# Second group's gate operands in four lots behind four outputs of the first group, its sums of squares behind the fourth and the spread behind the sixth, in a hybrid decoder step on one Trainium2 core

## The chip, the cores and the metric

The program runs on one core of a Trainium2 chip. The metric is the device time of one execution in microseconds (us). All data are float32; matrix products are made of three products of float32r pieces each (high times high, high times low, low times high), so that one float32 product of 128x128 weights costs three matmuls.

## What is computed

One layer of a hybrid decoder for 1024 new prompt tokens and 64 sample tokens. The change touches only its last part, the gated per-layer embedding:

```
gate = sigmoid(rmsnorm(x, g_ple) @ w_ple_gate)     # x: 1088 tokens x 1024, w_ple_gate: 1024 x 1024
x = x + gate * (p @ w_ple_proj)                    # p: 1088 x 256, w_ple_proj: 256 x 1024
```

The result x is an output of the step (y_prompt, y_sample).

## The kernel before

The tokens are held transposed (features on the partitions) in two groups: A with tokens 0 to 511 and B with tokens 512 to 1087 (576 tokens, two halves of 288). Each group has eight tiles of 128 features in `x`. rmsnorm is not applied to x itself: the gain goes into the operand, and 1/rms of each token (the row `rb`, spread over the partitions) is multiplied onto the product afterwards, in `gated` (L1599).

**Group A's gate.** `gate` (L1635) takes a slice of 256 output features at a time, four slices, two outputs (tiles of 128 features) each: 8 outputs. An output is 24 matmuls of 512 columns into one of three accumulator banks (0, 1, 2 in turn), then `gated`: 6 matmuls of the projection into bank 3 or 4 in turn (L1094 to L1096 with `ph`, `pl`), on VectorE the product with `rb` (L1603, which frees the accumulator bank), on ScalarE the sigmoid (L1604), on VectorE the product with the projection (L1605, which frees bank 3 or 4) and the sum into x (L1606). Last comes the store of the output before: four transposes on TensorE into bank 6 (L1615), a copy `yt` by ScalarE (L1616) and a DMA (L1617). The last slice's two outputs are made in halves of their inner dimension (L1638 to L1643).

**Group B's gate** (`gate7`, L1670) uses seven products of block sums instead of eight (`seven`, L1443). It needs operands made of B's x: four that are sums and differences of blocks (ids 2, 3, 1, 4; L1383 to L1399) and three direct ones (11, 21, 22; L1374 to L1382), and `rb` of B. For each k of 0 to 3 the four block operands cost two scalings on ScalarE (L1385, into `hk`), four subtractions on VectorE (L1390, L1392, L1394, L1396, into `tk`), four casts to the high piece on ScalarE (L1398) and four low pieces (L1399), two on VectorE and two on GpSimd (POOL). `rb` of B comes from `squares` (L1326: eight squares on ScalarE, three additions on POOL and three on VectorE, L1333, and one last one, L1334) and `spread` (L1337: products with a column of ones, L1345, square root, reciprocal, products that spread it, L1354). The direct operands are put where A's own operands `nh`, `nl` stood, so they wait for A's last matmul. `ple_inputs` (L1585) brings B's p: five DMAs `pn`, transposes (L1593), pieces `ph`, `pl` (L1596, L1597). `gate7_weights` (L1657) makes sums of weight blocks on VectorE (L1437 to L1440) and pieces of them (ScalarE L1074, then POOL or VectorE L1075).

**What sets the order.** The order on every engine comes from a list scheduler in the framework, which follows program order and its own estimates. The block `with tc.issue_after(end.ins)` (L1701) adds one rule: what is written in it for the engine of `end` (VectorE, the sum L1606 of output m) stands on that engine behind `end`. ScalarE's and POOL's instructions in the block are not bound by it. The loop of L1700 runs over the eight outputs of group A, m = 0 to 7, and hangs B's preparation behind them. Each engine works through its own list in order; SP issues the DMAs in its own list's order.

Of the kernel before, what the change touches and what calls it, by code (L numbers as in the profile page):

```python
# [48 lines left out]
def hybrid_step(ctx: ExitStack, tc: tile.TileContext, I, O):  # L49
# [17 lines left out]
    def banks(*ids):  # L67

        turn = itertools.cycle(ids)

        def take():
            i = next(turn)
            return psum.tile([128, 512], F32, name=f"b{i}", bufs=1)

        return take
# [152 lines left out]
    for s in range(2):  # L228
        hs = slice(64 * s, 64 * s + 64)
        for q in range(2):  # L230
            for kind in range(2):
                m = mfull[hs, q, kind, :]
# [1313 lines left out]
    mpb = tc.alloc_tile_pool(name="mlp_b", bufs=1, side="right", reuse_waits="tile")  # L1546
    B = Part(mpb, mpb, mpb, 512, 576, ((0, 288), (288, 288)))
# [14 lines left out]
    ops = B.operands("g_mlp", (2, 3, 1, 4), mpb, 4)  # L1562
# [22 lines left out]
    def ple_inputs(p, bank):  # L1585
        p.p = [[p.act(f"p{e}", F32R)] for e in "hl"]
        for i in p.tiles:
            r = 128 if i < 8 else NS
            t = B.tmp("pn")[:, :256]
            SP.dma_start(t[:r], pp_in[i * 128:i * 128 + 128, :] if i < 8 else ps_in)  # L1590
            pt = bank()
            for k in range(2):
                PE.transpose(pt[:, k * 128:k * 128 + r], t[:r, k * 128:k * 128 + 128], ident[:r, :r])  # L1593
            p3 = pt[:, :256].rearrange("p (k t) -> p k t", k=2)[:, :, :r]
            dst = slice(i * 128 - p.t0, i * 128 - p.t0 + r)
            S.copy(p.p[0][0][:, :, dst], p3)  # L1596
            V.tensor_sub(p.p[1][0][:, :, dst], p3, f(p.p[0][0][:, :, dst]))  # L1597
# [37 lines left out]
    def gate(p, sl):  # L1635
        w = load(wg_[:, sl * 256:sl * 256 + 256], 8, 256)
        w2_ = load(wp_[:, sl * 256:sl * 256 + 256], 2, 256)
        if sl == 3:  # L1638

            ps_ = [acc() for _ in range(2)]  # L1640
            for ks in (range(0, 4), range(4, 8)):
                for m2 in range(2):
                    gemm_p(ps_[m2], w, m2, p.h, 0, p.n, ks=ks)  # L1643
        for m2 in range(2):
            for t0, n in p.chunks:
                if sl == 3:
                    ps = ps_[m2]
                else:
                    ps = acc()
                    gemm_p(ps, w, m2, p.h, t0, n)  # L1650
                end = gated(p, w2_, m2, 2 * sl + m2, t0, n, ps[:, :n], B.tmp("g")[:, :n])
            finish(p, 2 * sl + m2)
            yield end
# [3 lines left out]
    def gate7_weights(sl, w):  # L1657

        s_ = [A.act("s", F32) for _ in range(2)]
        raw = [None] * 2 if sl % 2 == 0 else [B.act("wr", F32).rearrange("p a t -> p (a t)")[:, :1024] for _ in range(2)]  # L1660
        t = block_sums(wg_, sl * 256, [s_[i // 2][:, i % 2] for i in range(4)], raw)
        rp = raw_weights(wp_, 0, 2, sl * 256, 256, A.tmp("wr"))
        for n, i in enumerate((11, 2, 3, 1, 12, 4, 22) if sl else (2, 3, 1, 22, 11, 12, 4)):
            w[i] = split_piece(t[i], (G, V)[n % 2])
            if n == 6:
                w["p"] = Pieces(2)
                w["p"].hl[0, 0] = split_piece(rp, V)
            yield
# [30 lines left out]
    ops = {}  # L1699
    for m, end in enumerate(itertools.chain.from_iterable(gate(A, sl) for sl in range(4))):  # L1700
        with tc.issue_after(end.ins):  # L1701
            if m < 3:
                B.operands("g_ple", (2, 3, 1, 4), mpb, 4, ks=((0, 1), (2,), (3,))[m], out=ops)
            if m == 2:
                sums = B.squares()
            if m == 4:
                B.spread(sums, banks(3, 4))
                ple_inputs(B, banks(5, 7))
        if m == 6:
            w = {}  # L1710
            pieces = gate7_weights(0, w)
            for _ in range(5):
                next(pieces)
# [38 lines left out]
```

## Time and profile before

| | us |
|---|---|
| median of 3 runs | 1703.72 |
| lowest and highest run | 1699.27, 1712.79 |
| the profiled execution, its own time | 1706.69 |
| span of its trace, first to last instruction | 1705.1 |
| TensorE busy in the span | 1637.8 |

The span is the profiled execution from its first to its last instruction; 1.6 us of the execution's time lie outside it. Times in the trace count from the start of the span. TensorE (PE) rows give a matmul's busy time; matmuls overlap by a part, so the distance from start to start is what one costs: 0.23 us for 512 columns at the full clock. POOL is GpSimd, DVE is VectorE, ACT is ScalarE. A number in brackets behind a row is the time for which the engine stood idle just before it, with what ended that.

### The profile page before, as it was taken

To read this page: it belongs to the slowest core of one execution; us is meant where nothing else is said; L and a number is where in the kernel's file an instruction comes from. 1 tells how busy PE (TensorE), PEld (TensorE's weight loads), DVE (VectorE), ACT (ScalarE), POOL (GpSimd) and SP (SyncE) were. 2 spreads that over 40 slices of the span, in tenths; PEclk is the share of its full clock that TensorE was granted. 3 is DMA by queue.
4 is the path that set the end of the run, shared out by engine and by line. 5 is a ranking of instruction groups with operands and counts; after the bars stand their busy time and mean duration, and the time that the engine had idled before them with its cause. 6 is when DMAs were issued, how large, how long until landed. Compare 5 with 4: busy or idle time off the path is not lost.

```text
span 1705.1 us, 30847 instructions
## 1 busy us (share of the span) xinstructions
PE 1637.8 (96%) x11853; PEld 1476.2 (87%) x11853; DVE 1105.0 (65%) x1918; ACT 820.7 (48%) x1627; POOL 727.3 (43%) x778
## 2 busy tenths in 40 slices
PE   6999899999899889999999999999999999999898
PEld 5899888889898767888887778987999999999698
DVE  6266844555277759888854345378777777764986
ACT  6633433343343657666543444364444334436753
POOL 4123121123232664443434654366655445538621
PEclk9999999999999999999999999999999999999999
DMA  5134466325523763433245665322322222323232
GB/s 189 49 120 124 142 166 178 72 78 158 160 66 96 226 170 124 137 121 116 78 121 149 187 178 189 112 84 77 97 90 87 87 87 90 98 76 105 87 120 56
DMA packets 212372, 202.26 MB, mean 119 GB/s; under 512 B 58305, under 2 KB 177761, under 8 KB 212098
## 3 DMA queue, kind: packets, MB, share of 16 engines
q1 hardware_dynamic: 202498, 179.33, 35.4%
q0 software_dynamic: 5120, 16.78, 3.3%
q10 hardware_dynamic: 4608, 4.20, 1.0%
q8 instruction: 93, 1.52, 0.4%
q14 instruction: 53, 0.43, 0.1%
HBM read 163.27 MB, written 36.98 MB: 117 GB/s over the span
## 4 chain that ended last, share of the span: by engine, by line
PE 76%; DVE 10%; DMA 6%; ACT 3%; issue 3%; SPq 2%; POOL 1%; ACTq 0%; DVEq 0%; POOLq 0%
PE b L1094 12%; PE b L1096 11%; PE b L1095 11%; PE b L1453 4%; PE b L1455 4%; PE b L1454 4%; PE b L169 3%; PE b L170 3%; PE b L171 3%; PE b L797 2%; PE b L795 2%; PE b L796 2%; PE b L942 2%; DMA wr<-in_w_in 1%; PE b L512 1%
## 5 line engine op out<-in xcount | busy, mean ns | idle before, releaser
L1075 POOL TENSOR_TENSOR wl<-wr,wh 128x512 fp32r<-128x512 f32 x182 | 255.1, 1411 | 265.5 <-ACT wh L1074 226.3
L1074 ACT CAST wh<-wr 128x512 fp32r<-128x512 f32 x308 | 187.9, 621 | 308.9 <-PE b L1095 198.0
L1522 DVE TENSOR_TENSOR x<-b,x 128x288 f32<-128x288 f32 (+1 forms) x384 | 199.2, 528 | 97.2 <-PE b L1096 86.0
L1094 PE MATMUL b<-ah,wh 128*128 128x288 f32 (+1 forms) x768 | 253.7, 331 | 3.2 <-DVE x L1522 2.1
L1096 PE MATMUL b<-ah,wl 128*128 128x288 f32 (+1 forms) x768 | 252.2, 328 | 0.0
L1095 PE MATMUL b<-al,wh 128*128 128x288 f32 (+1 forms) x768 | 252.0, 328 | 0.0
L1094 PEld LDWEIGHTS b<-ah,wh 128*128 128x128 f32 x768 | 144.5, 188 | 15.3 <-DVE x L1522 4.8
L1096 PEld LDWEIGHTS b<-ah,wl 128*128 128x128 f32 x768 | 144.5, 188 | 10.2
L1095 PEld LDWEIGHTS b<-al,wh 128*128 128x128 f32 x768 | 144.6, 188 | 9.3 <-DVE al L1426 0.3
L1094 PE MATMUL b<-nh,wh 128*128 128x512 f32 x320 | 129.1, 403 | 5.4 <-DVE x L1413 3.3
L795 PE MATMUL b<-wh,h_hi 128*128 128x256 f32 x432 | 127.4, 295 | 5.1 <-ACT sq L805 5.1
L1095 PE MATMUL b<-nl,wh 128*128 128x512 f32 x320 | 128.1, 400 | 0.0
L1096 PE MATMUL b<-nh,wl 128*128 128x512 f32 x320 | 127.7, 400 | 0.0
L797 PE MATMUL b<-wh,h_lo 128*128 128x256 f32 x432 | 126.8, 293 | 0.0
L796 PE MATMUL b<-wl,h_hi 128*128 128x256 f32 x432 | 124.7, 289 | 0.0
L1075 DVE TENSOR_TENSOR wl<-wr,wh 128x512 fp32r<-128x512 f32 x126 | 102.4, 815 | 26.4 <-ACT wh L1074 22.4
L159 POOL TENSOR_TENSOR wl<-wr,wh 128x1024 fp32r<-128x1024 f32 x26 | 64.6, 2500 | 123.0 <-ACT wh L158 118.0
L169 PE MATMUL b<-h_hi,wh 128*128 128x384 f32 (+1 forms) x336 | 115.1, 342 | 1.9 <-ACT xs L333 1.3
L170 PE MATMUL b<-h_lo,wh 128*128 128x384 f32 (+1 forms) x336 | 113.8, 339 | 0.3 <-DVE h_lo L201 0.3
L171 PE MATMUL b<-h_hi,wl 128*128 128x384 f32 (+1 forms) x336 | 112.5, 335 | 0.0
L922 DVE TENSOR_TENSOR_SCAN keep<-keep,onesq 128x128 f32<-128x128 f32 (+3 forms) x64 | 95.3, 1488 | 21.4 <-POOL keep L920 20.7
L1453 PE MATMUL b<-op,wh 128*128 128x288 f32 x320 | 95.0, 297 | 0.1
(437 smaller groups left out, 4450.6 us busy)
## 6 DMA issues: line engine op xcount, KB each, us to landing
wr<-in_w_up SPq DMA_DIRECT2D x64, 512.0 KB
wr<-in_w_down SPq DMA_DIRECT2D x64, 512.0 KB
wr<-in_w_in SPq DMA_DIRECT2D x26, 512.0 KB
wr<-in_w_out SPq DMA_DIRECT2D x16, 512.0 KB
wr<-in_w_ple_gate SPq DMA_DIRECT2D x16, 512.0 KB
xt<-in_x_prompt SPq DMA_DIRECT2D x8, 512.0 KB
stk_s<-sth ACTq DMA_DIRECT2D x32, 128.0 KB
stk_s<-stl SPq DMA_DIRECT2D x32, 128.0 KB
```

Of the source, the lines that this page charges most:

```text
L169: PE.matmul(ps[:, :n], wh[:, k, c], a, start=(k == 0), stop=False)
L170: PE.matmul(ps[:, :n], wh[:, k, c], b, start=False, stop=False)
L171: PE.matmul(ps[:, :n], wl[:, k, c], a, start=False, stop=(k == nk - 1))
L795: PE.matmul(o, a, w[0][:, k, :], start=(k == 0), stop=False)
L797: last = PE.matmul(o, b, w[0][:, k, :], start=False, stop=(k == 7))
L1074: S.copy(h3, src)
L1075: (sub or G).tensor_sub(l3, src, f(h3))
L1094: PE.matmul(ps[:, :n], w(0, k, m), a, start=(k == 0), stop=False)
L1095: PE.matmul(ps[:, :n], w(0, k, m), b, start=False, stop=False)
L1096: PE.matmul(ps[:, :n], w(1, k, m), a, start=False, stop=(k == nk - 1))
L1453: PE.matmul(o, wh[:, k], x[:, 0, k], start=k == 0, stop=False)
L1522: V.tensor_add(p.x[:, m, t0:t0 + n], ps[:, :n], p.x[:, m, t0:t0 + n])
```

## The change

Two things move in the loop over group A's outputs. The block operands of B for k = 0, 1, 2, 3 were written behind outputs 0 (k = 0 and 1), 1 and 2; now each k has an output of its own, 0 to 3. B's squares move from output 2 to output 3, and the spread and B's p from output 4 to output 5. Outputs are numbered from 0 here and below.

```
-            if m < 3:
-                B.operands("g_ple", (2, 3, 1, 4), mpb, 4, ks=((0, 1), (2,), (3,))[m], out=ops)
-            if m == 2:
+            if m < 4:
+                B.operands("g_ple", (2, 3, 1, 4), mpb, 4, ks=(m,), out=ops)
+            if m == 3:
                 sums = B.squares()
-            if m == 4:
+            if m == 5:
                 B.spread(sums, banks(3, 4))
                 ple_inputs(B, banks(5, 7))
```

Three places where the scheduled order differs follow. Numbers behind b are those of a bank's use: before, outputs 2, 3, 4, 5, 6, 7 accumulate in b_18273, b_18352, b_18423, b_18524, b_18595, b_18596; now outputs 2, 3, 5 have b_18257, b_18318, b_18468, and outputs 4, 6, 7 the same names as before.

VectorE from output 3's product with `rb` to output 4's, before (b_18378 is output 3's projection, tk belongs to the lot k = 3, s is a sum of weight blocks):

```order
L1603 TENSOR_TENSOR g<-b_18352,rb 128x512
L1399 TENSOR_TENSOR op_18151<-tk,op_18151 128x288
L1399 TENSOR_TENSOR op_18153<-tk,op_18153 128x288
L1333 TENSOR_TENSOR sums<-sums,sq 128x576
L1437 TENSOR_TENSOR s<-wr 128x512
L1439 TENSOR_TENSOR s<-wr 128x512
L1333 TENSOR_TENSOR sums<-sums,sq 128x576
L1605 TENSOR_TENSOR g<-b_18378,g 128x512
L1438 TENSOR_TENSOR s<-s,wr 128x512
L1333 TENSOR_TENSOR sums<-sums,sq 128x576
L1606 TENSOR_TENSOR x<-x,g 128x512
L1603 TENSOR_TENSOR g<-b_18423,rb 128x512
```

The same place now (b_18344 is output 3's projection):

```order
L1603 TENSOR_TENSOR g<-b_18318,rb 128x512
L1399 TENSOR_TENSOR op_18150<-tk,op_18150 128x288
L1605 TENSOR_TENSOR g<-b_18344,g 128x512
L1606 TENSOR_TENSOR x<-x,g 128x512
L1390 TENSOR_TENSOR tk<-hk 128x288
L1396 TENSOR_TENSOR tk<-hk 128x288
L1392 TENSOR_TENSOR tk<-hk,tk 128x288
L1394 TENSOR_TENSOR tk<-hk,tk 128x288
L1437 TENSOR_TENSOR s<-wr 128x512
L1333 TENSOR_TENSOR sums<-sums,sq 128x576
L1439 TENSOR_TENSOR s<-wr 128x512
L1399 TENSOR_TENSOR op_18151<-tk,op_18151 128x288
```

Output 3's L1605 and L1606 now stand two and three places behind its L1603 instead of seven and ten; the lot k = 3, the sums of squares and the weight sums come behind them.

TensorE at the store of output 2 (b_18389 before, b_18355 now; b_18449 is output 4's projection), before:

```order
L1094 MATMUL b_18524<-nh_17988,wh 128x512
L1095 MATMUL b_18524<-nl_17990,wh 128x512
L1096 MATMUL b_18524<-nh_17988,wl 128x512
L1615 MATMUL b_18389<-ident,x 128x128 x4
L1094 MATMUL b_18524<-nh_17988,wh 128x512
L1095 MATMUL b_18524<-nl_17990,wh 128x512
```

And now:

```order
L1096 MATMUL b_18449<-ph,wl 128x512
L1094 MATMUL b_18449<-ph,wh 128x512
L1615 MATMUL b_18355<-ident,x 128x128 x4
L1095 MATMUL b_18449<-pl,wh 128x512
L1096 MATMUL b_18449<-ph,wl 128x512
L1094 MATMUL b_18468<-nh_17988,wh 128x512
```

The store stands 11 matmuls earlier: inside output 4's projection instead of behind the first nine matmuls of output 5.

TensorE at the products of the spread with the column of ones (b_18469 before, b_18514 now; b_18561 and b_18505 are the store of output 4), before:

```order
L1094 MATMUL b_18596<-nh_17988,wh 128x512
L1095 MATMUL b_18596<-nl_17990,wh 128x512
L1345 MATMUL b_18469<-onesq,sums 128x1 x5
L1096 MATMUL b_18596<-nh_17988,wl 128x512
L1615 MATMUL b_18561<-ident,x 128x128 x4
L1593 MATMUL b_18491<-ident,pn 128x128 x2
```

And now:

```order
L1096 MATMUL b_18596<-nh_17988,wl 128x512
L1345 MATMUL b_18514<-onesq,sums 128x1 x2
L1615 MATMUL b_18505<-ident,x 128x128 x4
L1345 MATMUL b_18514<-onesq,sums 128x1 x3
L1094 MATMUL b_18596<-nh_17988,wh 128x512
L1095 MATMUL b_18596<-nl_17990,wh 128x512
```

Before, the products stand behind 11 matmuls of output 7, and output 5's six projection matmuls come only later; now they stand behind 6 matmuls of output 7, with output 5's projection already done, and the transposes of p come later.

## Rows read from the trace of the kernel before

**Rows 1.** The head of the page: the span, and each engine's busy time, share and instructions.

```profile
span 1705.1 us, 30847 instructions
PE 1637.8 (96%) x11853; PEld 1476.2 (87%) x11853; DVE 1105.0 (65%) x1918; ACT 820.7 (48%) x1627; POOL 727.3 (43%) x778
```

**Rows 2.** Waits of PE from 1545 us to the end: engine, line, what it waited for, us in total, times, longest us.

```profile
PE b L1615 <- DVE x L1606: 3.6, 2, 2.5
PE b L1615 <- ACT yt L1616: 2.6, 1, 2.6
PE b L1345 <- DVE g L1605: 2.3, 1, 2.3
```

**Rows 3.** Busy time by stretch: stretch, its length, then busy us and instructions of PE, weight loads, DVE, ACT and POOL, the granted clock of PE as a share of full speed, DMA share, GB/s.

```profile
1577.50:1592.70 15.20, 15.20 (x71) 12.57 (x70) 14.05 (x18) 10.48 (x20) 9.62 (x8) 1.00 0.27 87
1592.70:1618.90 26.20, 18.80 (x87) 14.65 (x85) 25.99 (x31) 18.63 (x37) 18.89 (x13) 1.00 0.31 91
1618.90:1637.00 18.10, 18.05 (x90) 15.97 (x91) 13.12 (x28) 12.09 (x25) 3.28 (x2) 0.81 0.47 149
1637.00:1680.00 43.00, 43.00 (x326) 42.47 (x325) 41.08 (x78) 22.72 (x47) 15.45 (x11) 1.00 0.27 77
```

**Rows 4.** PE by time (start us, us, instruction, idle before): the three standstills, a matmul of 512 columns behind the last of them, one later, and two of 288 columns.

```profile
1604.02 0.66 PE L1615 MATMUL b<-ident,x 128*128 128x128 f32 x4 [2.64 <-ACT yt L1616]
...
1613.31 0.63 PE L1615 MATMUL b<-ident,x 128*128 128x128 f32 x4 [2.46 <-DVE x L1606]
...
1618.95 1.87 PE L1345 MATMUL b<-onesq,sums 128*128 128x1 f32 x10 [2.35 <-DVE g L1605]
...
1623.39 0.63 PE L1095 MATMUL b<-nl,wh 128*128 128x512 f32 x1
...
1632.55 0.29 PE L1455 MATMUL b<-op,wl 128*128 128x288 f32 x1
1632.69 0.29 PE L1453 MATMUL b<-op,wh 128*128 128x288 f32 x1
```

**Rows 5.** The chain of waits that ended last, its pieces just ahead of the spread (start us, us, what).

```profile
1614.77 1.85 DVE sums L1334
1616.62 1.67 DVE wl L1075
1618.29 0.61 DVE g L1605
...
1618.95 1.87 PE b L1345 x10
```

**Rows 6.** DVE by time: instructions on SBUF tensors alone and beside POOL, then the two products and the sum that finish output 3.

```profile
1583.20 0.45 DVE L1396 TENSOR_TENSOR tk<-hk 128x288 f32<-128x288 f32 x1
...
1584.17 1.54 DVE L1390 TENSOR_TENSOR tk<-hk 128x288 f32<-128x288 f32 x1
...
1603.34 0.68 DVE L1603 TENSOR_TENSOR g<-b,rb 128x512 f32<-128x512 f32 x1
...
1609.94 0.75 DVE L1333 TENSOR_TENSOR sums<-sums,sq 128x576 f32<-128x576 f32 x1
1610.61 0.68 DVE L1605 TENSOR_TENSOR g<-b,g 128x512 f32<-128x512 f32 x1
...
1612.48 0.68 DVE L1606 TENSOR_TENSOR x<-x,g 128x512 f32<-128x512 f32 x1
```

**Rows 7.** POOL by time at the place of the second row of rows 6, then two of its groups by line between 1594.4 and 1617.8 us (busy us, mean ns, idle before and its releasers).

```profile
1583.67 3.19 POOL L1075 TENSOR_TENSOR wl<-wr,wh 128x512 fp32r<-128x512 f32 x2 [1.31 <-ACT wh L1074]
...
L1075 POOL TENSOR_TENSOR wl<-wr,wh 128x512 fp32r<-128x512 f32 x4 | 6.4, 1602 | 2.5 <-ACT wh L1074 2.5
L1399 POOL TENSOR_TENSOR op<-tk,op 128x288 fp32r<-128x288 f32 x4 | 4.2, 1074 | 0.0
```

**Rows 8.** ACT by time: a table load ahead of a sigmoid, a sigmoid, the third cast of the lot k = 3, a square, and the copy `yt` of output 1's store.

```profile
1577.98 1.28 ACT L1604 ACT_TABLE_LOAD   x1
...
1592.86 0.63 ACT L1604 ACTIVATE g<-g 128x512 f32<-128x512 f32 x1 [1.06 <-DVE g L1603]
...
1602.48 0.43 ACT L1398 CAST op<-tk 128x288 fp32r<-128x288 f32 x1 [0.53 <-DVE tk L1396]
1602.82 0.68 ACT L1331 ACTIVATE sq<-x 128x576 f32<-128x576 f32 x1
1603.40 0.56 ACT L1616 COPY yt<-b 128x512 f32<-128x512 f32 x1
```

**Rows 9.** SP by time: the loads of the weights that L1437 and L1439 sum.

```profile
1599.73 1.83 SPq L1068 DMA_DIRECT2D wr<-in_w_ple_gate  x2
```

**Rows 10.** Busy time by stretch, columns as in rows 3: two other places where the granted clock fell.

```profile
629.00:637.00 8.00, 4.75 (x14) 3.76 (x15) 4.09 (x4) 4.72 (x9) 8.00 (x6) 0.79 0.24 76
...
901.00:907.40 6.40, 5.53 (x37) 4.49 (x37) 1.11 (x2) 2.40 (x6) 2.37 (x3) 0.73 0.68 221
```

**Rows 11.** DVE by time behind the spread: the last direct operand, a weight sum, and output 6's product with `rb`.

```profile
1630.53 1.81 DVE L1380 SCALAR_TENSOR_TENSOR op<-x,par,op 128x288 fp32r<-128x288 f32 x4 [3.59 <-ACT op L1379]
1632.25 0.69 DVE L1437 TENSOR_TENSOR s<-wr 128x512 f32<-128x512 f32 x1
1632.85 0.69 DVE L1603 TENSOR_TENSOR g<-b,rb 128x512 f32<-128x512 f32 x1
```

## Prediction, made before the changed kernel had run

> **What bounds the kernel now.** I read the head of the page, then PE's waits in the last part, then busy time by stretch, then the chain of waits and the single engines' timelines. PE is busy for 1637.8 of 1705.1 us [rows 1], so over the whole span PE is the bound, and the change can only win where PE stands still or runs slowly. Around the change PE waits four times; three of the waits lie where group A's gate is computed: 2.64, 2.46 and 2.35 us [rows 2, 4], 7.45 us together. By stretch [rows 3], PE is full from 1577.5 to 1592.7, busy 18.80 of 26.20 us from there to 1618.9, full again behind that but with a granted clock of 0.81 for 18.1 us, which costs 0.19 x 18.1 = 3.4 us, and full at full clock from 1637 to 1680. That is what there is to win: 7.45 + 3.4 = 10.9 us, 0.6% of the time.
>
> In the stretch of the standstills another engine is full: DVE, 25.99 of 26.20 us [rows 3]. The chain of waits runs along DVE there and reaches PE through the last sum of squares (L1334), a weight piece and output 4's L1605, behind which the spread's first product starts at 1618.95 [rows 5]. So the stage is set by DVE up to that point, and PE's standstills are what is left over.
>
> **What DVE's time is made of.** In those 26.2 us DVE runs 29 instructions of interest: 13 of 288 columns (five L1399, eight subtractions), 12 of 512 (two L1603, three L1605, two L1606, four weight sums, one L1075) and 4 of 576 (three L1333, one L1334). Alone, one of 288 columns takes some 0.37 us from start to start (the L1396's 0.45 of rows 6 less the 0.07 by which a row's end overlaps the next start, as for L1605: 0.68 there, 0.61 in rows 5), one of 512 thus 0.61, one of 576 0.67 (L1333 to L1605 in rows 6). That is 13 x 0.37 + 12 x 0.61 + 4 x 0.67 = 14.8 us. The other 11.4 us are time in which DVE waits for POOL inside an instruction: an instruction on two SBUF tensors takes 1.54 instead of 0.45 us when POOL is in one of its own [rows 6, 7], and POOL is busy 18.89 us here with 13 instructions [rows 3].
>
> **The change part by part.** Nothing is added or removed; it is all order. Up to 1592.7 nothing moves on any engine: the lots k = 0 and 1 already ran together, because outputs 0 and 1 end together, and they still do.
>
> Between 1592.7 and the spread the same 29 DVE instructions and the same 13 of POOL run as before, only sorted differently. So the time at which DVE is through with L1334 and output 4's L1605 moves only by what DVE idles and by how the POOL waits fall. I find two new idles: output 2's and output 3's L1605 now follow their L1603 with a single L1399 (0.4 us) between, while the sigmoid between them takes 0.63 us [rows 8] and some 0.1 us of hand-over, so 0.35 us each, 0.7 us. The other waits on ACT are covered: the casts of the lot k = 3 stand behind four squares (4 x 0.6 us) on ACT, but DVE has two weight sums and an addition ahead of the L1399 that needs them. If that cover were gone it would cost those 2.4 us. From below, if the waits for POOL fell away, L1334 could be earlier by up to 11.4 us, but then PE's own work is the bound and the gain ends at 7.45. I take +0.7, by the nearest rows: DVE is full before and has no less to do.
>
> Where PE stands still moves. Walking the rows on: output 2's L1606 ends near 1596, and the copy of output 1's store on ACT comes behind the casts of one lot alone, near 1600 instead of 1603.4 [rows 8], so PE, which reaches the store of output 2 at 1598.7, waits some 1.5 instead of 2.64 us there. Output 3's L1605 and L1606 run near 1603 instead of 1610.6 and 1612.5 [rows 6], so the store of output 3 no longer waits for them (2.46 us), but for the copy of the store before it, which stands behind the squares and the lot's casts on ACT, near 1609: 1.5 us. Then 20 matmuls of 0.23 us and the store bring PE to the spread near 1614, and L1334 lets it in near 1619.6: some 5 us in one piece. The sum of the waits is what it was, because its end is fixed by DVE. PE has done one matmul of 512 columns more at that point (6 of output 5's projection against 5 of output 7): -0.2 us. Net +0.5 us.
>
> [...] It fell behind two waits of 2.4 us with a store and 11 matmuls between. At two other places a single standstill brought it down for a cost of 0.21 x 8 and 0.27 x 6.4 us, 1.7 us each [rows 10]. So one standstill of 5 us costs 1.7 to 3.4; I keep 3.4, no change, because PE restarts on the same single-column products and transposes. [...]
>
> Behind the spread PE was full before, so anything new there is a loss. The spread's products of L1354 stand 21 matmuls behind L1345, the square root and reciprocal fit in that. On SP the first weight load of L1437 can leave earlier than 1599.7 [rows 9], the second stands behind the store of output 1 and leaves near 1600.7, as before; DVE needs them near 1607. The loads of B's p now stand behind two weight loads that wait for DVE's weight pieces, near 1622.5; PE needs them near 1628. Cover is 3 us. Zero for all of this, up to 2 us if one cover fails.
>
> Sum: +0.7 - 0.2 + 0 + 0 = +0.5 us on the profiled execution's 1706.7, so 1707.2. The median of the runs is 3.0 us below that execution, and the same step on it gives 1704.2 us.
>
> **The rivals.** First, a gain: the lots fall so that DVE waits less for POOL. For it: DVE's five instructions on PSUM do not wait for POOL (0.68 us in every row of them [rows 6]), and now stand nearer to the lots; 11.4 us of waiting are there to shrink. Against it: the same 13 POOL instructions hang on the same casts. Every us off goes to PE, to -7.4, and with the clock kept up -10.9; in the middle -5, 1698.7. [...]
>
> Second, a loss behind the spread. The product b_18821 of the second group now comes early and needs bank 0, which output 7 holds until its L1603. On DVE that L1603 now stands behind the four last direct operands and two weight sums, and those operands may not be written before PE's last gate matmul, since they go where A's operands are. From that matmul DVE needs 0.2 + 1.8 + 3 x 0.6 = 3.8 us with ACT free at once [rows 11], and PE has 12 matmuls of 0.23 us, 24 of 0.13 and two groups of four transposes, some 0.5 each, 6.9 us [rows 4]. So it decides from the point at which ACT comes 3 us late to those operands; DVE has stood 3.59 us for it at that place before [rows 11]. In ACT's list two copies of rb, two pieces of p, a table load and a sigmoid stand there (0.9 + 0.7 + 1.3 + 0.6 and hand-overs, some 3.9 us; the last two [rows 8], the copies and pieces by their sizes) while PE does nine matmuls (2.1 us): 1.8 us late, near the edge. At 5 to 8 us late PE loses 2 to 5 us: 1708.0. If PE's clock stays up, PE comes 1.7 to 3.4 us earlier and this wait takes that back.
>
> Third, nothing changes but the place, my forecast without its +0.7: 1703.7, not to be told apart.
>
> **How the numbers follow.** Forecast with the third rival, within 3 us: 0.58. Gain of 3 to 11 us: 0.22. Loss of 3 to 7 us: 0.20. The likeliest is 1704.2. Its own range is 1701 to 1707; gain and loss reach from 1693 to 1711. The runs before spread over 1699.3 to 1712.8, and the median of a few moves by some 3 us. I leave out the end of the gain: 1697 to 1711. One per cent, about what a measurement of this kernel can tell from no change, is 17 us: a gain of that size is more than there is to win (0.01), a loss of it needs several waits of rows 2 at once (0.03), so 0.96 within.
>
> **What would show it.** In the profile of the changed kernel PE's waits should be two near 1.5 us at the stores of outputs 2 and 3, and one near 5 us ahead of L1345; DVE full from 1593 to 1619; L1345 within 1.5 us of 1619; a clock near 0.8 behind it; PE full from 1640 to 1680. Wrong is the step on DVE if L1345 starts before 1616 with POOL as busy as before, and the step behind the spread if PE stands at bank 0.

## The result, and the profile after

The changed kernel takes 1710.43 us (median of 20 runs, 1707.0 to 1714.8); the kernel before, run beside it, 1707.13 us (20 runs, 1699.3 to 1712.8). The ratio is 1.0020, 95% interval 1.0012 to 1.0029: 2 to 5 us slower, some 3.4 us. That is inside the range (1697 to 1711) and inside "within 1%", but on the side of the second rival.

The page of the changed kernel begins so [rows 1]:

```profile
span 1711.5 us, 30847 instructions
PE 1640.7 (96%) x11853; PEld 1477.6 (86%) x11853; DVE 1106.6 (65%) x1918; ACT 822.4 (48%) x1627; POOL 726.5 (42%) x778
```

The 6.4 us between the two spans are not all the change's. Output 2's product with `rb` (L1603), ahead of which no engine's list differs, starts at 1595.82 us here and at 1592.14 before. So distances from that instruction are compared, not times from the start:

| | output 2's L1603 to L1345 | L1345 to the end | together |
|---|---|---|---|
| before | 26.81 | 86.15 | 112.96 |
| after | 26.94 | 88.74 | 115.68 |

Up to the spread 0.13 us are lost, behind it 2.59 us. PE's waits from 1545 us to the end (engine, line, what it waited for, us in total, times, longest), against [rows 2]:

```profile
PE b L1345 <- DVE sums L1334: 5.7, 1, 5.7
PE b L1615 <- ACT yt L1616: 1.5, 2, 1.1
PE b L1453 <- DVE c L1603: 1.3, 1, 1.3
PE b L1615 <- DVE x L1606: 1.1, 1, 1.1
PE b L1453 <- DVE pl L1597: 0.6, 1, 0.6
```

The L1606 of 1.1 us is the end of the program and was part of the 3.6 us of [rows 2]. Ahead of L1345 the three waits of 7.45 us have become 1.5 and 5.7, 7.2 us. The two waits at L1453 are new; they stand in the second group's first slice. By stretch (columns as in [rows 3]: PE, weight loads, DVE, ACT, POOL, granted clock, DMA):

```profile
1596.40:1622.60 26.20, 19.15 (x88) 14.71 (x86) 25.73 (x30) 16.56 (x32) 18.46 (x13) 0.96 0.27 81
1622.60:1640.70 18.10, 17.94 (x84) 15.55 (x85) 12.24 (x25) 14.35 (x29) 2.28 (x2) 0.78 0.54 164
1640.70:1683.70 43.00, 41.11 (x309) 40.28 (x308) 41.23 (x77) 21.66 (x46) 15.30 (x12) 1.00 0.26 77
```

The first row is the stage of the standstills: DVE full, POOL as busy as before. Its clock of 0.96 is a fall that began while PE still stood ahead of L1345, as the stretch of that standstill alone shows (PE busy 0.00 us, clock 0.80):

```profile
1617.02:1622.76 5.74, 0.00 (x1) 0.00 (x1) 5.74 (x6) 2.10 (x5) 4.46 (x3) 0.80 0.19 49
```

The second row has the clock at 0.78 where it was 0.81. The third was full before (43.00 of 43.00 [rows 3]) and has lost 1.89 us. PE by time shows all the places (start us, us, instruction, idle before it):

```profile
1603.63 0.66 PE L1615 MATMUL b<-ident,x 128*128 128x128 f32 x4 [1.06 <-ACT yt L1616]
...
1611.54 0.66 PE L1615 MATMUL b<-ident,x 128*128 128x128 f32 x4 [0.41 <-ACT yt L1616]
...
1622.76 1.01 PE L1345 MATMUL b<-onesq,sums 128*128 128x1 f32 x4 [5.74 <-DVE sums L1334]
...
1644.44 0.34 PE L1593 MATMUL b<-ident,pn 64*128 64x64 f32 x2
...
1650.68 0.40 PE L1453 MATMUL b<-op,wh 128*128 128x288 f32 x1 [0.63 <-DVE pl L1597]
...
1658.09 0.40 PE L1453 MATMUL b<-op,wh 128*128 128x288 f32 x1 [1.26 <-DVE c L1603]
```

The row at 1644.44 transposes the last tile of B's p into bank 5. The row at 1650.68 is the first product into bank 5 behind it, and it waits until DVE has made that tile's low piece (L1597). DVE by time between the two:

```profile
1640.53 1.03 DVE L1437 TENSOR_TENSOR s<-wr 128x512 f32<-128x512 f32 x1 [0.99 <-DMA wr<-in_w_ple_gate]
1641.48 0.68 DVE L1439 TENSOR_TENSOR s<-wr 128x512 f32<-128x512 f32 x1
...
1645.74 1.78 DVE L1440 TENSOR_TENSOR s<-wr,s 128x512 f32<-128x512 f32 x1
1647.44 1.77 DVE L1075 TENSOR_TENSOR wl<-s,wh 128x512 fp32r<-128x512 f32 x1
1649.14 0.68 DVE L1606 TENSOR_TENSOR x<-x,g 128x512 f32<-128x512 f32 x1
1649.74 0.68 DVE L1075 TENSOR_TENSOR wl<-s,wh 128x512 fp32r<-128x512 f32 x1
1650.35 0.28 DVE L1597 TENSOR_TENSOR pl<-b,ph 128x128 fp32r<-128x128 f32 x1
...
1652.58 1.31 DVE L1682 TENSOR_TENSOR u<-b,u 128x288 f32<-128x288 f32 x3 [1.35 <-PE b L1455]
...
1657.59 0.81 DVE L1603 TENSOR_TENSOR c<-b,rb 128x288 f32<-128x288 f32 x2
```

The small L1597 runs 5.9 us after its transpose, behind a weight sum, two weight pieces and the end of an output, two of them 1.8 instead of 0.68 us long. In the kernel before, DVE ran it 1.4 us after its transpose (PE at 1637.54):

```profile
1636.52 0.68 DVE L1440 TENSOR_TENSOR s<-wr,s 128x512 f32<-128x512 f32 x1
...
1637.72 0.68 DVE L1075 TENSOR_TENSOR wl<-s,wh 128x512 fp32r<-128x512 f32 x1
...
1638.92 0.28 DVE L1597 TENSOR_TENSOR pl<-b,ph 128x128 fp32r<-128x128 f32 x1
```

A weight sum and a weight piece stood ahead of it there too; one weight piece more does now. Beyond that DVE as a whole comes late: it starts L1437 17.8 us behind L1345, before 13.3 [rows 11], and the two slow rows, which run beside POOL's own weight pieces, cost 2.2 us more than at 0.68 each.

The last row of DVE above (L1603 at 1657.59) is the second wait: it reads the bank that the next product needs. DVE first stands 1.35 us until the product that L1597 held up is done (L1682 at 1652.58), and then has weight sums of the next slice ahead of the L1603. Those stood ahead of it in the kernel before too, where PE does not wait:

```profile
1645.75 0.68 DVE L1437 TENSOR_TENSOR s<-wr 128x512 f32<-128x512 f32 x1
...
1647.68 1.73 DVE L1438 TENSOR_TENSOR s<-s,wr 128x512 f32<-128x512 f32 x1
1649.33 0.81 DVE L1603 TENSOR_TENSOR c<-b,rb 128x288 f32<-128x288 f32 x2
```

So their place in the list alone is not the cause of the second wait.

### The profile page after: what moved, and what is told of

Read it like the earlier page. It is cut to its first block, busy times and chain, and to the rows that moved or that the text cites. A ratio compares the mean times of both kernels' runs of the same rounds, so it can differ in the third digit from the quotient of the medians.

```text
span 1711.5 us, 30847 instructions
## 1 busy us (share of the span) xinstructions
PE 1640.7 (96%) x11853; PEld 1477.6 (86%) x11853; DVE 1106.6 (65%) x1918; ACT 822.4 (48%) x1627; POOL 726.5 (42%) x778
## 4 chain that ended last, share of the span: by engine, by line
PE 77%; DVE 10%; DMA 5%; issue 3%; ACT 3%; SPq 1%; POOL 1%; DVEq 0%; ACTq 0%; POOLq 0%
PE b L1094 12%; PE b L1096 12%; PE b L1095 12%; PE b L1453 4%; PE b L1455 4%; PE b L1454 4%; PE b L169 3%; PE b L170 3%; PE b L171 3%; PE b L797 2%; PE b L795 2%; PE b L796 2%; PE b L942 2%; DMA wr<-in_w_in 1%; PE b L512 1%
## 5 line engine op out<-in xcount | busy, mean ns | idle before, releaser
L1075 DVE TENSOR_TENSOR wl<-wr,wh 128x512 fp32r<-128x512 f32 x126 | 103.0, 819 | 27.6 <-ACT wh L1074 25.2
L1453 PE MATMUL b<-op,wh 128*128 128x288 f32 x320 | 95.2, 297 | 2.0 <-DVE c L1603 1.3
```

Source lines behind the costliest of these rows:

```text
L1075: (sub or G).tensor_sub(l3, src, f(h3))
L1453: PE.matmul(o, wh[:, k], x[:, 0, k], start=k == 0, stop=False)
```

## The experiments

The question is which part of the change costs the 2.6 us behind the spread, and by what. Theory 1: the spread and p, one output later, are late for what follows. Rivals: the smaller lots or the squares; the loads in SP's list; DVE being late everywhere for POOL's sake. All were run in 5 rounds beside the kernel before; a ratio is to that kernel, with its 95% interval in brackets. "Distances" are the two of the table above, from one profile each.

**The lots and the squares as changed, the spread and p back behind output 4** (e1, from the changed kernel).

```diff
-            if m == 5:
+            if m == 4:
                 B.spread(sums, banks(3, 4))
                 ple_inputs(B, banks(5, 7))
```

> The changed kernel with only the spread and B's p put back behind output 4 (lots behind 0 to 3 and squares behind 3 stay). The changed kernel was 1.002 of before; in its profile the distance from output 2's L1603 to the spread's first product (L1345) is 26.9 us against 26.8 before, and from L1345 to the end 88.7 against 86.2. Theory 1 (the loss lies behind the spread: B's p and the weight loads behind it on SP come an output later, VectorE idles there and runs into group B with a backlog): the loss goes, ratio 0.999 to 1.001, no wait of TensorE between 1640 and 1665, L1345 to the end 86 to 87 us. Theory 2 (the lots and squares are the cause, the spread only shows it): ratio stays 1.0015 to 1.003.

Ratio 1.0008 (0.9997 to 1.0019). Distances 26.97 and 86.51 us: of the 2.59 us behind the spread 0.36 are left, PE's waits at L1453 are gone, and the granted clock over the 18.1 us from L1345 is 0.81 again. It is the profile that shows this; the ratio's interval overlaps that of the changed kernel (1.0012 to 1.0029).

**The spread and p alone one output later** (e2, from the kernel before).

```diff
-            if m == 4:
+            if m == 5:
                 B.spread(sums, banks(3, 4))
                 ple_inputs(B, banks(5, 7))
```

> The kernel before with only the spread and B's p moved from output 4 to output 5; lots and squares as before. Theory 1: nearly the whole loss, ratio 1.001 to 1.003, one or two waits of TensorE in group B's first slice, L1345 to the end 88 us or more. Theory 2: no loss, ratio 0.999 to 1.001.

Ratio 1.0012 (1.0002 to 1.0023), as theory 1 had it. Distances 26.82 and 86.72 us, where theory 1 had 88 or more. Behind the spread the clock was granted in full (1.00 over the 18.1 us from 1620.6; 3.4 us less to pay there than before), and new waits took it back: 0.7 us for `pn`, and this one of the second group's first slice, without any wait for L1597 (PE's waits):

```profile
PE b L1453 <- DVE c L1603: 2.2, 1, 2.2
```

**The four lots alone** (e3, from the kernel before).

```diff
-            if m < 3:
-                B.operands("g_ple", (2, 3, 1, 4), mpb, 4, ks=((0, 1), (2,), (3,))[m], out=ops)
+            if m < 4:
+                B.operands("g_ple", (2, 3, 1, 4), mpb, 4, ks=(m,), out=ops)
```

> The kernel before with only the lots spread over outputs 0 to 3; squares behind output 2 and spread behind 4 stay. Theory 1: 0.999 to 1.001, and from output 2's L1603 to L1345 26 to 28 us, since VectorE and GpSimd do the same work in that stretch in any order. Theory 2: 1.001 to 1.003. If the lots themselves helped (less waiting of VectorE for GpSimd), L1345 would come 2 us or more earlier and the ratio would be 0.998 or less.

Ratio 0.9993 (0.9981 to 1.0005), distances 26.79 and 84.98 us. The lots cost nothing that shows; with e1, the loss goes with the place of the spread and p. One wait is new here, for output 6's L1603, which stands on DVE behind the last direct operands and weight sums, as the second rival had it for output 7's (PE by time):

```profile
1635.80 0.40 PE L1453 MATMUL b<-op,wh 128*128 128x288 f32 x1 [0.73 <-DVE g L1603]
```

**POOL's share of the second group's preparation on VectorE** (e4, from the kernel before; `alone` is filled ahead of the loop over the outputs).

```diff
-                    (G, V)[m % 2].tensor_add(sums[:, m % 2], sums[:, m % 2], t)
+                    (V if alone else G, V)[m % 2].tensor_add(sums[:, m % 2], sums[:, m % 2], t)
-                    (V, G)[(a + k) % 2].tensor_sub(out[i][:, 1, k], val[i], f(out[i][:, 0, k]))
+                    (V, V if alone else G)[(a + k) % 2].tensor_sub(out[i][:, 1, k], val[i], f(out[i][:, 0, k]))
-            w[i] = split_piece(t[i], (G, V)[n % 2])
+            w[i] = split_piece(t[i], (V if sl == 0 else G, V)[n % 2])
```

> The kernel before with GpSimd's share of B's preparation given to VectorE: the eight low pieces L1399, the three additions of squares and the weight pieces of group B's first slice. The prediction's account of VectorE (14.8 us of its own and 11.4 us of waiting for GpSimd in the 26.2 us up to the spread): VectorE gets 4 x 0.37 + 3 x 0.67 + 3 x 0.61 = 5.3 us more and waits some 0.6 x 14.5 = 8.7 us less, so L1345 comes about 3.4 us earlier and the time is 0.998 of before. Rival (GpSimd's work is mostly free, since VectorE waits for other things): L1345 comes 5 us later, ratio 1.002 to 1.004.

Ratio 0.9968 (0.9954 to 0.9983), distances 21.77 and 85.58 us. From output 2's L1603 to L1345 (columns as above):

```profile
1592.50:1614.30 21.80, 21.43 (x99) 17.17 (x99) 21.80 (x39) 16.94 (x35) 4.91 (x3) 1.00 0.32 97
```

DVE has 8 instructions more than before and is through 5.0 us earlier (3.4 were expected), with POOL busy 4.9 instead of 18.9 us; PE is full (21.43 of 21.80), and its clock is 1.00 here and in the 18.0 us behind. Three more low pieces stand ahead of output 2's product in this list, so 5.0 us is if anything too little: counted from the first store of group A, L1345 comes 6.4 us earlier.

**p back behind output 4, the spread as changed** (e5, from the changed kernel).

```diff
+            if m == 4:
+                ple_inputs(B, banks(5, 7))
             if m == 5:
                 B.spread(sums, banks(3, 4))
-                ple_inputs(B, banks(5, 7))
```

> The changed kernel, with B's p (its five loads, transposes and pieces) put back behind output 4; lots, squares and the spread (behind output 6) as changed. Distance from output 2's L1603 to L1345: 26.8 to 27.1 us in either theory. Theory 1a (the loss behind the spread comes from the spread itself one output later: the direct operands and what DVE has queued behind them start later, and PE overtakes DVE in group B's first slice): the distance from L1345 to the end stays at 88 to 89 us, ratio to the kernel before 1.0015 to 1.0025. Theory 1b (it comes from p: its loads and the weight loads behind them on SP's queue run 5 to 10 us late, and DVE and PE wait for those): the distance goes back to 86 to 86.7 us, ratio 0.9995 to 1.0008, and the weight load of B's first slice leaves before 1630 us.

**p alone one output later** (e8, from the kernel before).

```diff
             if m == 4:
                 B.spread(sums, banks(3, 4))
+            if m == 5:
                 ple_inputs(B, banks(5, 7))
```

> The kernel before, with B's p alone put one output later; lots, squares and spread as before. Distance from output 2's L1603 to L1345: 26.6 to 27.0 us. Theory 1a (the spread costs it): no loss, the distance from L1345 to the end stays at 85.5 to 86.5 us and the ratio at 0.9995 to 1.0005. Theory 1b (p costs it): 1 to 2 us of new waits of PE in group B's first slice (at the transposes of p and at the products that need its pieces or the weights loaded behind them), distance 87 to 88 us, ratio 1.0005 to 1.0015.

e5: ratio 1.0021 (1.0009 to 1.0034), distances 26.93 and 87.43 us. e8: 1.0021 (1.0008 to 1.0034), distances 26.80 and 89.14 us. Neither of the two theories holds alone: either step costs, each by another thing. With p back (e5) the new waits are gone, and the weight loads leave at 1621.7 us as 1b had it; but the standstill of 5.7 us ahead of L1345 is there, and the clock behind it is lower than in any other run (by stretch, from L1345):

```profile
1618.70:1636.70 18.00, 18.00 (x84) 15.87 (x85) 13.84 (x27) 13.76 (x28) 2.09 (x2) 0.74 0.48 151
```

0.26 x 18.0 = 4.7 us against 3.4 before, +1.3: that is all of the 87.43 less 86.15. With p late and the old waits (e8) the clock is 0.81 as before, and two waits of the changed kernel's kinds are new, 2.7 us of the 3.0 (PE by time, then DVE):

```profile
1641.08 0.34 PE L1593 MATMUL b<-ident,pn 64*128 64x64 f32 x2
...
1642.76 0.37 PE L1453 MATMUL b<-op,wh 128*128 128x288 f32 x1 [0.59 <-DVE pl L1597]
...
1654.96 0.40 PE L1453 MATMUL b<-op,wh 128*128 128x288 f32 x1 [2.09 <-DVE c L1603]
```

```profile
1642.20 0.41 DVE L1597 TENSOR_TENSOR pl<-b,ph 128x256 fp32r<-128x256 f32 x1
```

The L1597 waited for is that of p's fourth tile (bank 7), not of its last: it ends just ahead of 1642.76, and the last tile's runs at 1643.74.

**The changed kernel with POOL's share on VectorE** (e6: e4's edit on the changed kernel), and **the four lots with it** (e7: e4's edit on e3).

> The changed kernel, with GpSimd's share of the second group's preparation on VectorE (half of the subtractions L1399, half of the additions L1333, and the weight pieces of the second group's first slice). Kernel before with the same edit: distance from output 2's L1603 to L1345 21.8 us, ratio 0.997. If VectorE's time ahead of the spread is the sum of its own work and POOL's share of it, whatever the order, the distance is 21.5 to 22.5 us here too. Theory 1 (the change costs behind the spread only): L1345 to the end 87 to 89 us, ratio to the kernel before 0.998 to 0.9995, so 1.5 to 3 us slower than the kernel before with this edit. Rival (the change costs only because VectorE is late everywhere, POOL's share being part of that backlog): 85 to 86.5 us, ratio 0.9955 to 0.9975, as the kernel before with this edit or faster.

> The kernel before with the operands in four lots behind four outputs (squares behind output 2 of 0 to 7, spread and p behind output 4, as before), and GpSimd's share of the second group's preparation on VectorE. Distance from output 2's L1603 to L1345: 21.3 to 22.3 us. Lots alone gave 85.0 us behind L1345, and GpSimd's share moved alone 85.6. If both edits add up: ratio 0.995 to 0.9965, the fastest of all orders. Rival (PE is full and both edits take the same standstills): 0.9965 to 0.998, as the kernel before with GpSimd's share on VectorE.

e6: ratio 0.9984 (0.9969 to 0.9999), distances 29.09 and 83.85 us, 112.94 together where e4 has 107.35. The time is as theory 1 had it, the two distances are not: PE, not DVE, now comes last to the spread (busy 27.96 of 29.10 us there), so L1345 is late by its place in PE's list. Behind it PE stands 2.1 us for the reciprocal of L1350 (L1348 before that edit), 0.9 for `pn` and 1.8 at the two places of the second group's first slice (lines are two higher in these kernels). PE's waits in e6:

```profile
PE b L1356 <- DVE rs L1350: 2.1, 1, 2.1
PE b L1455 <- DVE c L1605: 1.3, 1, 1.3
...
PE b L1595 <- DMA pn<-in_p_prompt: 0.9, 1, 0.9
PE b L1455 <- DVE pl L1599: 0.5, 1, 0.5
```

The clock is 0.81 over the 18.1 us from L1345, where it is 1.00 in e4; that is 3.4 of the 5.6 us between the two. So the change costs with DVE relieved too, in the profiles more than before; by the intervals of the ratios the difference to e4 stays open.

e7: ratio 0.9958 (0.9942 to 0.9975), median 1697.90 us, distances 23.37 (expected 21.3 to 22.3) and 85.42 us. It is the fastest version run, faster than both kernels, and not to be told apart from e4.

**B's five loads of p issued by GpSimd instead of SP**, in the changed kernel (e9) and in e8 (e10).

```diff
-            SP.dma_start(t[:r], pp_in[i * 128:i * 128 + 128, :] if i < 8 else ps_in)
+            (G if p is B else SP).dma_start(t[:r], pp_in[i * 128:i * 128 + 128, :] if i < 8 else ps_in)
```

> The changed kernel with B's five loads of p issued by GpSimd instead of SP; the order of TensorE, VectorE and ScalarE is that of the changed kernel, SP's differs by these five loads alone. Theory 1c (the loads of p and the weight loads behind them stand in SP's one list behind weight loads that wait for VectorE, and that makes the new waits): p's transposes and the weight sum L1437 stand earlier, the two new waits of PE in group B's first slice (0.63 and 1.26 us) fall to under 0.5 together, L1345 to the end 87.0 us or less (88.7 in the changed kernel), ratio to the kernel before 1.0005 to 1.0015. Rival 1d (the list of SP is only later because VectorE and TensorE are: the buffers pn and wr come free late): waits and distance stay, 88 to 89 us, ratio 1.0015 to 1.0025; POOL's share may add some 0.5 us.

> The kernel before with B's p one output later and its five loads issued by GpSimd. With SP's loads PE had two new waits of 2.7 us together in group B's first slice, and L1345 to the end was 89.1 us. Theory 1c: waits under 1.2 us, 86 to 87.5 us, ratio 0.9995 to 1.0010. Rival 1d: waits 2 to 3 us, 88.5 to 89.5 us, ratio 1.0015 to 1.0025.

e9: ratio 1.0017 (1.0007 to 1.0027), distances 26.92 and 88.79 us. e10: 1.0022 (1.0008 to 1.0036), distances 26.79 and 88.93 us. Theory 1c falls, twice. In e9 the weight loads leave at 1627.7 instead of 1634.9 us, DVE no longer idles for them, and PE's new waits are what they were (DVE by time in e9):

```profile
1639.52 0.68 DVE L1437 TENSOR_TENSOR s<-wr 128x512 f32<-128x512 f32 x1
1640.12 1.77 DVE L1439 TENSOR_TENSOR s<-wr 128x512 f32<-128x512 f32 x1
...
1650.10 0.28 DVE L1597 TENSOR_TENSOR pl<-b,ph 128x128 fp32r<-128x128 f32 x1
```

And PE's waits:

```profile
PE b L1453 <- DVE c L1603: 1.3, 1, 1.3
PE b L1615 <- DVE x L1606: 1.1, 1, 1.1
PE b L1453 <- DVE pl L1597: 0.7, 1, 0.7
```

So the loads' place in SP's list is not the cause. That the idle of 0.99 us did no harm is not shown by it: in its place L1439 takes 1.77 instead of 0.68 us, and DVE comes to the last L1597 27.9 us behind L1345, in the changed kernel 27.6.

**p two outputs later** (e11, from the kernel before).

```diff
+            if m == 6:
                 ple_inputs(B, banks(5, 7))
```

> The kernel before with B's p two outputs later (behind output 6), all else as before. One output later gave 2.7 us of new waits and 89.1 us from L1345 to the end. If each output's delay adds the like, since the slack ahead of the first product with p is used up: 5 to 6 us of waits, 91 to 93 us, ratio 1.003 to 1.0045. Rival (the waits come from how p's pieces fall between the second group's first products and VectorE's weight pieces, not from their lateness): no more than with one output, 86 to 89.5 us, ratio 0.9995 to 1.002.

Ratio 1.0052 (1.0036 to 1.0068), distances 26.79 and 96.08 us: 7 us more than with one output, above what either side expected. The wait for DVE's L1603 grows, and PE now waits for p's load and for the copy of a store too (PE's waits behind L1345):

```profile
PE b L1453 <- DVE c L1603: 3.2, 1, 3.2
...
PE b L1593 <- DMA pn<-in_p_prompt: 1.9, 1, 1.9
...
PE b L1615 <- ACT yt L1616: 0.7, 1, 0.7
PE b L1455 <- POOL wl L1075: 0.3, 1, 0.3
```

The new waits, 6.1 us, are more than half of the 9.9 us to the kernel before; the clock fell twice more there, at 1642 and 1659 us (0.92 over the 43 us from 1635.9, some 3 us).

## Why the prediction was right or wrong

**The number: inside the range, but not by the sum.** The sum was +0.5 us, the runs have +3.4. The median of 1710.4 us is 6.2 above the likeliest 1704.2: 3.4 of that are the kernel before, whose median is 1707.1 with 20 runs and was 1703.7 with three, and 2.8 are the change. The forecast's own range (1701 to 1707) does not hold it; the wide one, made for the rivals, does by 0.6 us, and that is luck. (The third rival's 1703.7 is the median before; the sum without its +0.7 gives 1703.5.)

**DVE's account ahead of the spread: right.** The distance to L1345 was to grow by 0.5 us and grew by 0.13. In the eight other kernels with POOL's share in place it is 26.8 to 27.0 us as well. They are fewer orders than kernels: ahead of L1345 DVE's list is that of the kernel before in e2, e8, e10 and e11, that of the changed kernel in e1, e5 and e9, and a third one in e3. In these three the first rival (DVE waits less for POOL) got nothing from order. That DVE pays for POOL was shown by taking POOL's share away: 5.0 us, although DVE then does that work itself.

**PE's standstills: right in kind, their split off.** Forecast were 1.5, 1.5 and about 5 us; they are 1.06, 0.41 and 5.74. The copies `yt` on ACT come earlier than I had walked them. The sum hardly moved, 7.2 for 7.45 us, because its end is fixed by DVE.

**The clock: mis-sized by 0.5 us.** I kept 3.4 us and took 1.7 to 3.4 as bounds. It is 0.22 x 18.1 = 4.0 us here, and 4.7 in e5. The granted clock had fallen behind the short standstills as well, as the trace of before said: it is 0.50 there for 6.8 us (1619.45 to 1626.27), with 0.43 us from one matmul of 512 columns to the next. With the joined one it is 0.50 for 10.2 us here (1620.40 to 1630.65) and, in windows of 1 us, for as long in e5. Of the two other places, from which I had the 1.7, one has a standstill of 3.34 us; at the other PE stood three times, for 0.41 to 0.65 us, so it does not show what one standstill costs. With what passed while PE still stood ahead of L1345, the fall amounts to 5.0 us here (1.0 and 4.0) and 5.2 in e5 (0.5, at 0.98 over the 26.9 us ahead, and 4.7), so the two are alike and differ in how much of it passed in the standstill. In e1, where the same standstill is in two parts (1.3 and 4.4 us), the clock is 0.81 again. By these rows the joining cost 0.5 to 1.3 us.

These are single executions. Each run also lists the mean granted clock of its span; what is missing to 1, times the span, is 24.2 us in the mean of the changed kernel's 20 runs and 20.8, 21.3 and 21.5 us in the three sets of runs of the kernel before beside the experiments (83 in all). That is some 3 us more, part of which passes in standstills and costs nothing. So the clock may weigh more in the 3.4 us of the runs than the 0.5 us of the one profile.

**Behind the spread: the term that failed.** It stood at zero, "up to 2 us if one cover fails". It is 1.89 us of waits in the changed kernel and 2.7 in e8. Two things were wrong in it. I looked at whether p's loads come in time, and PE never waited for them in the changed kernel; in e9 and e10 the loads come from another queue and the waits stay. And I ended the walk at the transposes and did not follow the banks on. The smaller wait is for L1597, which reads a tile of p out of its bank (0.63 us for the last tile here, 0.59 for the fourth in e8). The larger is for the L1603 of the second group's first slice (1.26 us here, 2.1 in e8, 2.2 in e2, 3.2 in e11); in e2 and e11 it stands without the smaller one. DVE comes late to both: with p later, it starts L1437 15.3 to 28.6 us behind L1345 (the changed kernel, e2, e8 to e11), with p in its old place 10.9 to 13.3 us (before, e1, e3, e5). e1, which leaves p and the spread in their old place, has neither wait; e8, which moves p alone, has both.

**The second rival: the right kind, the wrong place.** A product of the second group that comes to a bank before DVE is through with it, behind weight sums, is what happened; the bank was 5 (and then that of an L1603 of the first slice), not bank 0 with output 7's L1603. Its price of 2 to 5 us holds the 2.7 us of the distances by luck, since the new waits are 1.9 us. A wait for an L1603 of group A, as it had it, is in e3 (0.7 us) and e4 (1.2 us), not in the changed kernel. By one sign that I had written, "wrong is the step behind the spread if PE stands at bank 0", the step would have passed; by another, PE full from 1640 to 1680, it failed (41.11 of 43.00 us).

**The ledger.** Waits behind the spread +1.9, clock +0.5, ahead of the spread +0.1: 2.5 of the 2.7 us in the profiles. By their middle values the parts do not add up: p late alone (e8) and the spread late alone (e5) each give 1.0021, both together 1.0012 on the old lots (e2) and 1.0020 on the new. The intervals are too wide to say more.

**What stays open.** e5's profile has 1.4 us, its runs 1.5 to 5.8. The clocks of its 12 runs go with that: they lose 24.2 us against 21.3 in the runs beside them. In e2 the clock's gain (3.4) and the new waits (2.9) leave a distance of -0.5 us, and it is +0.6. The clock fell there too, but ahead of the spread (0.94 from output 2's L1603 to L1345), where DVE sets the time. In e11 it is 0.94 there as well, though every engine's list up to that fall is the one of the kernel before, which had 1.00; why it fell earlier was not tried. Nor was a kernel that moves the L1597 or the L1603 alone ahead in DVE's list, or one in which DVE reaches the second group's weight sums as early as before. So the runs show that p's and the spread's place cost the time, while the order in DVE's list, DVE's lateness as a whole and its slow rows beside POOL are not told apart; their part in the two waits rests on the rows.

## What to carry to other kernels

A step that is moved later must be followed to the last reader of every bank and buffer it takes, and to where the engine of that reader then is in its list, not to the arrival of its data: here reads of 0.3 to 0.4 us, to which a busy engine came late, held up the engine that bounds the kernel for 1.9 us. Where one engine's work slows another's (two of DVE's rows took 1.8 for 0.68 us beside POOL's), three orders of their work gave the same time here (26.8 to 27.0 us), and giving the work to one of them gained 5 us (21.8). Before joining several short waits into one, look at what the clock does behind each: here it fell either way, and was 0.50 for 10.2 us with the joined one, for 6.8 us behind the short ones. An idle row that a change removes can come back as a slow row behind it (e9: an idle of 0.99 us went, and L1439 took 1.77 instead of 0.68 us), so look at when the engine arrives, not at the idle.

## What the runs showed of the hardware

- Moving 14 us of POOL's busy time to DVE made DVE's stage 5.0 us shorter, 21.8 for 26.8 us, with 8 instructions more on DVE (e4).
- The granted clock behind standstills of 7.2 to 7.5 us in all averaged 0.81 over 18 us after three of 2.4 to 2.6 us, 0.78 and 0.74 after 1.06, 0.41 and 5.74 us: the same waits, in the changed kernel and in e5, cost 4.0 and 4.7 us, and 5.0 and 5.2 with what passed before PE went on. With PE full to the spread (e4) it stayed at 1.00.
- Behind the same instructions on TensorE and VectorE, output 2's L1603 started at 1587.98 (e10), 1592.14 (before) and 1595.82 us (changed): 7.8 us between executions, more than the change is worth. Distances inside the stage repeated to 0.2 us in ten kernels (26.8 to 27.0 us).
